# Hybrid decoder layer: the gate projection by Strassen's scheme and ahead of the attentions, and branch products beside branch A's attention

## The chip, the cores and the metric

The kernel runs on one core of a Trainium2 chip. TensorE (PE) multiplies, VectorE (DVE) and ScalarE (ACT) do element-wise work, GpSimd (POOL) and SyncE (SP) issue transfers here. The metric is device time in microseconds (us) of one launch, median of the runs. Program text that sets the order is Python: it writes one list of instructions for each engine, and an engine runs its list in that order.

## What is computed

One layer for 512 tokens and a model width of 2048, all float32. Cut to what matters here:

```python
h = rms_norm(x, norm_g)
(aq, ak, av, az, iq, ik, iw, bcq, bckv, bkpe, bz, cq, cz, gates) = split(h @ w_in)
o_a = dsa_attention(...)     # top 128 of the causal keys by an indexer, 8 heads, relative bias
o_b = mla_attention(...)     # low-rank queries and keys, 8 heads
o_c = memory_attention(...)  # 4 heads over 256 memory tokens, keys from rms_norm(mem) @ w_mem_kv
u = stack([o_a * silu(az), o_b * silu(bz), o_c * silu(cz)])      # each 512 x 1024
y_br = einsum('bsnw,nwd->bsnd', u, w_branch)                     # three products 1024 -> 2048
g = sigmoid(gates.reshape(512, 3, 2048))
merged = einsum('bsnd,bsnd->bsd', g, y_br)
x = x + merged @ w_out
```

The gates are the largest part of the input projection: 2048 x 6144.

## The kernel before

Every large product is made three times: both factors are split into a high and a low part of 12 bits (`split`, line 242: ACT makes the high half, DVE the low one), and high x high, low x high and high x low are summed in PSUM. Such a product is a row of PE of 128x128 by 512 columns. `hh` and `hl` are the halves of h, `whi` and `wlo` those of weights, `uh` and `ul` those of the gated branch outputs, `mh` and `ml` those of the merged sum.

The work of PE is a stream (`stream`, line 259) of chunks; a chunk is 512 columns of one weight matrix, with four PSUM banks of the ring `pg`. For each block k of 128 rows it has 4 x 3 products. SP's queue loads the weights (`wraw`, two blocks of k to a load, 512 KB), and the splits run `LOOK` = 5 blocks ahead. The order of the chunks is written in `build` (line 1269): memory keys and values, latents, queries of C, up-projections of B, keys and values of A, the indexer's queries, queries of A, twelve gate chunks, then three times (branches C, B, A) two chunks of the gate path (`z_chunk`) and four of the branch product (`branch_chunk`), then the output projection.

Between the products of the stream, threads emit the steps of norms and attentions. `run` (line 350) keeps an estimate of every engine's clock: a step is emitted once the products emitted so far outlast what it waits for. A chunk can name a flag (`need`); the stream stops until that flag is set. The first gate-path chunk needs flag "A", the end of branch A's attention. `defer` (line 344) puts element-wise work of a finished chunk a few groups of products later.

A gate chunk's banks are taken out of PSUM by ACT as tanh(x/2), since sigmoid(x) = (1 + tanh(x/2)) / 2, and stored in DRAM (`tanh_to_dram`). `z_chunk` multiplies silu(z) with the attention output, loaded from DRAM, and splits the result into `uh` and `ul`, which stay in SBUF. `branch_chunk` loads the chunk's gates (`y_g`), multiplies them with the bank and adds up the branches in `m`; columns of the weights are on partitions, so after branch A the sum is split as it stands and enters the output projection.

POOL issues all transfers but the weights' loads, in the order in which they are written. Helper lines: every operation goes through a wrapper, so the profile gives all of them line L138; they are told apart by the names of their tiles.

Of the kernel before, what the change touches and what calls it, by code (L numbers as in the profile page):

```python
# [51 lines left out]
PE = object()  # L52


class Engine:
    """An engine's namespace whose calls also advance an estimate of when each tile is written: the
    order in which steps are emitted follows it."""
# [14 lines left out]
class Plan:  # L72
    """Estimated clocks of the engines and of the tiles."""
# [9 lines left out]
    def cost(self, kind, name, out, aps, accum):  # L83
# [3 lines left out]
        if kind == "pe":  # L87
            if name == "transpose":
                return 108
            if aps[1].dtype == BF:  # L90
                return 0.417 * n + 1
            return max(0.417 * n + 2, 108) if n >= 128 else 214
# [59 lines left out]
class Slots:  # L152
    """A tile pool whose tags rotate, with an estimate of when the next slot of a tag is free."""
# [42 lines left out]
class Core:  # L196
    """The core with its engines watched by a plan."""
# [13 lines left out]
def bc(ap, shape, axis):  # L211
    """A broadcast view: a new axis of stride 0."""
    return ap.unsqueeze(axis).to_broadcast(shape)


class Kern:
    LOOK = 5
# [6 lines left out]
    # ---------------------------------------------------------------- helpers  # L224
# [5 lines left out]
    def rsqrt(self, pool, y, v, n):  # L230
        """y = v ** -0.5 on [128, n] (v normal, positive): seed and three Newton steps."""
# [10 lines left out]
    def split(self, hi, lo, src, gain=None):  # L242
        """hi + lo = src * gain, each of 12 bits."""
# [8 lines left out]
    # ---------------------------------------------------------------- the stream of products  # L252
    def chunk(self, w, nk, cols, act, mode, nb, evac, need=None):
        """One block of columns of a product: w [nk*128, cols] in DRAM (or a list of its pieces),
        act(kt) the split activations [128, tokens]. mode "tm": tokens on partitions; "fm": columns on partitions."""
        self.chunks.append(dict(w=w if isinstance(w, list) else [w], nk=nk, cols=cols, act=act, mode=mode,
                                nb=nb, evac=evac, need=need))

    def stream(self):
# [4 lines left out]
        units, loads, lidx = [], [], {}  # L264
        for ci, c in enumerate(self.chunks):
            for k in range(c["nk"]):
                if k % 2 == 0:
                    loads.append((ci, k))
                lidx[ci, k] = len(loads) - 1
                units.append((ci, k))  # L270
        raw, hl = {}, {}
        nload = nsplit = 0

        def load_upto(n):
            nonlocal nload
            while nload < min(n, len(loads)):
                ci, k = loads[nload]
                c = self.chunks[ci]
                r = self.wp.tile([P, 2, 512], F32, name="wraw", tag="wraw", bufs=self.NRAW)
                c0 = 0  # L280
                for w in c["w"]:
                    c1 = c0 + w.shape[1]
                    nc.sync.dma_start(r[:, :, c0:c1], w[k * P:(k + 2) * P, :].rearrange("(k p) c -> p k c", p=P))
                    c0 = c1
                raw[nload] = r
                nload += 1

        def split_upto(n):
            nonlocal nsplit
            while nsplit < min(n, len(units)):  # L290
                ci, k = units[nsplit]
                j = lidx[ci, k]
                load_upto(j + self.NRAW)
                w = self.chunks[ci]["cols"]
                h = self.wp.tile([P, 512], F32R, name="whi", tag="whi", bufs=6)
                l = self.wp.tile([P, 512], F32R, name="wlo", tag="wlo", bufs=6)
                self.split(h[:, :w], l[:, :w], raw[j][:, k % 2, :w])
                hl[ci, k] = (h, l)
                nsplit += 1

        for i, f in enumerate(self.first_loads):
            f()
            load_upto(min(i + 1, self.NRAW))
        yield "boot"

        for i, (ci, k) in enumerate(units):
            c = self.chunks[ci]
            split_upto(i + 1 + min(self.LOOK, i))
            need = c["need"](k) if callable(c["need"]) else c["need"]
            while need and need not in self.flags:  # L310
                yield "stall"
            if k == 0:
                if c.get("pre"):
                    c["pre"]()
                c["ps"] = [self.pg.bank([P, 512]) for _ in range(c["nb"])]
            wh, wl = hl.pop((ci, k))
            ah, al = c["act"](k)
            s, e = k == 0, k == c["nk"] - 1
            for b in range(c["nb"]):
                p = c["ps"][b]  # L320
                if c["mode"] == "tm":
                    n = c["cols"]
                    sl = slice(b * P, (b + 1) * P)
                    mm(p[:, :n], ah[:, sl], wh[:, :n], start=s, stop=False)
                    mm(p[:, :n], ah[:, sl], wl[:, :n], start=False, stop=False)
                    mm(p[:, :n], al[:, sl], wh[:, :n], start=False, stop=e)
                else:
                    m = min(P, c["cols"] - b * P)
                    sl = slice(b * P, b * P + m)
                    mm(p[:m], wh[:, sl], ah, start=s, stop=False)  # L330
                    mm(p[:m], wh[:, sl], al, start=False, stop=False)
                    mm(p[:m], wl[:, sl], ah, start=False, stop=e)
                if e:
                    c["evac"](b, p)
                yield
# [8 lines left out]
    def defer(self, f, last, gap=1):  # L344
        """Do this later: once the chunk's last bank has been read, one after every gap groups of products."""
# [4 lines left out]
    def run(self, main, threads):  # L350
        """Threads yield what their next step waits for: tiles that have to be written, or the name of
        a flag. A step is emitted once the products emitted so far outlast that wait."""
# [25 lines left out]
        def force():  # L378
# [4 lines left out]
            assert c, "deadlock"  # L383
# [17 lines left out]
    # ---------------------------------------------------------------- constants on the chip  # L401
    def setup(self):
        nc, A = self.nc, self.A
        cp = self.cp
        self.g_m = cp.tile([P, KT], F32, name="g_m")
        jp = self.wp.tile([P, 512], I32, name="jp", tag="stage", bufs=5)[:, :P]
# [15 lines left out]
    def small_loads(self):  # L422
        """Gains and constants."""
# [23 lines left out]
    def rotary_tables(self, pool):  # L447
        """cos and sin of position * frequency, tokens on partitions; the position rows for branch A."""
# [126 lines left out]
    # ---------------------------------------------------------------- where the chunks go  # L575
# [4 lines left out]

    def to_dram(self, key, nb, cols, scale=None, sums=()):
        """Write the banks of a chunk to DRAM, [128, nb, cols]. sums: (from, to, dst): dst(b) [128, 1] =
        sum of squares of these columns."""
        nc = self.nc
        dt = self.spill_tile(key, nb, cols)

        def evac(b, p):
            st = self.wp.tile([P, 512], F32, name="stage", tag="stage", bufs=5)
            src, dst = p[:, :cols], st[:, :cols]
# [3 lines left out]
            elif scale is None:  # L593
                nc.vector.tensor_copy(dst, src)
            else:
                nc.vector.tensor_scalar(dst, src, sc, None, op0=OP.mult)
            nc.gpsimd.dma_start(dt[:, b], dst)
# [3 lines left out]
            def squares():  # L601
                for c0, c1, d in sums:
                    junk = self.wp.tile([P, 512], BF, name="junk", tag="junk")
                    nc.scalar.activation(junk[:, :c1 - c0], st[:, c0:c1], AF.Square, accum_out=d(b))
# [6 lines left out]
    def tanh_to_dram(self, key):  # L611
        nc = self.nc
        dt = self.spill_tile(key, 4, 512)

        def evac(b, p):
            st = self.wp.tile([P, 512], F32, name="stage", tag="stage", bufs=5)
            nc.scalar.activation(st, p, AF.Tanh, scale=0.5)
            nc.gpsimd.dma_start(dt[:, b], st)
# [828 lines left out]
```

## Time and profile before

| | |
|---|---|
| median of 3 runs | 1963.02 us (1962.42 to 1963.19) |
| span of the profiled execution | 1961.6 us |
| PE busy | 1946.4 us, 9757 matmuls |
| DVE busy | 1026.6 us |
| ACT busy | 765.9 us |
| data moved | 268.16 MB, mean 137 GB/s |

Busy time of PE counts matmuls that are pipelined, so their durations overlap; what a product costs is its distance from the next. Idle time of an engine that is not the bottleneck costs nothing.

### The profile page before, as it was taken

What the parts mean: (1) busy time and instruction counts of PE and PEld (TensorE: products, weight loads), DVE (VectorE), ACT (ScalarE), POOL (GpSimd) and SP (SyncE); (2) the same over time, 40 slices, a digit from 0 to 9 for tenths busy, and PEclk for the clock granted to TensorE, in tenths of its full rate; (3) what the DMA queues carried; (4) which work ended last, traced back from release to release, by engine and by line L of the source; (5) the groups of instructions that cost most, each with busy time, mean ns of one, the idle gap of its engine ahead of it and who ended that gap; (6) DMA issues with size and microseconds to landing.
All of it is one profiled execution on the core that took longest, in us unless ns stands there. A gap on an engine that the chain in (4) does not pass through costs nothing.

```text
span 1961.6 us, 26146 instructions
## 1 busy us (share of the span) xinstructions
PE 1946.4 (99%) x9757; PEld 1627.1 (83%) x9757; DVE 1026.6 (52%) x2108; ACT 765.9 (39%) x1605; POOL 160.3 (8%) x276
## 2 busy tenths in 40 slices
PE   8999999999999999999999999999999999999999
PEld 6789888888888888888888888888888888888887
DVE  5654425656556668956677652244334544464332
ACT  6644348444455543333333343233223323333221
POOL 1000003111111000020101100000000000000000
PEclk9999999999999999999999999999999999999999
DMA  8735447544344333344433334533433443444442
GB/s 274 241 113 156 132 124 245 166 145 140 108 135 129 116 106 121 112 139 120 128 103 106 116 99 118 162 117 120 162 119 118 139 163 108 128 137 142 141 140 78
DMA packets 121199, 268.16 MB, mean 137 GB/s; under 512 B 12704, under 2 KB 17552, under 8 KB 118512
## 3 DMA queue, kind: packets, MB, share of 16 engines
q1 hardware_dynamic: 99472, 186.80, 31.9%
q0 software_dynamic: 21568, 79.69, 11.9%
q8 instruction: 76, 1.25, 0.3%
q14 instruction: 51, 0.42, 0.1%
q10 hardware_dynamic: 32, 0.01, 0.0%
HBM read 224.74 MB, written 41.71 MB: 136 GB/s over the span
## 4 chain that ended last, share of the span: by engine, by line
PE 94%; DMA 2%; issue 1%; DVE 1%; ACT 1%; POOL 0%; ACTq 0%; POOLq 0%
PE pg L138 85%; PE pb L138 3%; PE pa L138 3%; PE ra L138 2%; DMA wraw<-w_mem_kv 2%; PE rb L138 1%; DVE wlo L138 1%; ACT whi L138 0%; DMA ikw<-sp_bckv 0%; DMA g_rows<-mem_norm_g 0%; ACT junk L138 0%; ACT memh L138 0%; DVE px L138 0%; DMA sp_oC<-c_o 0%; DVE stage L138 0%
## 5 line engine op out<-in xcount | busy, mean ns | idle before, releaser
L138 DVE TENSOR_TENSOR wlo<-wraw,whi 128x512 fp32r<-128x512 f32 (+2 forms) x680 | 461.8, 684 | 744.8 <-ACT whi L138 712.7
L138 ACT ACTIVATE whi<-wraw 128x512 fp32r<-128x512 f32 (+2 forms) x680 | 421.3, 625 | 887.3 <-PE pg L138 814.8
L138 PE MATMUL pg<-hh,whi 128*128 128x512 f32 x1280 | 510.6, 399 | 0.0
L138 PE MATMUL pg<-hh,wlo 128*128 128x512 f32 x1280 | 499.9, 391 | 0.0
L138 PE MATMUL pg<-hl,whi 128*128 128x512 f32 x1280 | 499.1, 390 | 0.0
L138 PEld LDWEIGHTS pg<-hh,wlo 128*128 128x128 f32 x1280 | 240.2, 188 | 51.7
L138 PEld LDWEIGHTS pg<-hl,whi 128*128 128x128 f32 x1280 | 240.9, 188 | 44.1
L138 PEld LDWEIGHTS pg<-hh,whi 128*128 128x128 f32 x1280 | 240.7, 188 | 44.0
L138 PE MATMUL pg<-whi,hh 128*128 128x512 f32 (+1 forms) x448 | 175.3, 391 | 0.4 <-DVE stage L138 0.4
L138 PE MATMUL pg<-whi,hl 128*128 128x512 f32 (+1 forms) x448 | 171.9, 384 | 0.0
L138 PE MATMUL pg<-wlo,hh 128*128 128x512 f32 (+1 forms) x448 | 171.6, 383 | 0.0
L138 PE MATMUL pg<-ul,whi 128*128 128x512 f32 x384 | 149.4, 389 | 0.0
L138 PE MATMUL pg<-uh,whi 128*128 128x512 f32 x384 | 149.4, 389 | 0.0
L138 PE MATMUL pg<-uh,wlo 128*128 128x512 f32 x384 | 149.4, 389 | 0.0
L138 PE MATMUL pg<-wlo,mh 128*128 128x512 f32 x256 | 99.6, 389 | 0.0
L138 PE MATMUL pg<-whi,mh 128*128 128x512 f32 x256 | 99.6, 389 | 0.0
L138 PE MATMUL pg<-whi,ml 128*128 128x512 f32 x256 | 99.6, 389 | 0.0
L138 PEld LDWEIGHTS pg<-whi,hl 128*128 128x128 f32 x448 | 84.1, 188 | 15.5
L138 PEld LDWEIGHTS pg<-whi,hh 128*128 128x128 f32 x448 | 84.3, 188 | 14.3 <-DVE stage L138 0.9
L138 PEld LDWEIGHTS pg<-wlo,hh 128*128 128x128 f32 x448 | 84.3, 188 | 13.1
L138 PEld LDWEIGHTS pg<-uh,whi 128*128 128x128 f32 x384 | 72.1, 188 | 15.0
L138 PEld LDWEIGHTS pg<-ul,whi 128*128 128x128 f32 x384 | 72.1, 188 | 14.9
(343 smaller groups left out, 2366.1 us busy)
## 6 DMA issues: line engine op xcount, KB each, us to landing
wraw<-w_in SPq DMA_DIRECT2D x208, 512.0 KB, 3.6
wraw<-w_branch SPq DMA_DIRECT2D x48, 512.0 KB, 3.7
wraw<-w_mem_kv SPq DMA_DIRECT2D x32, 512.0 KB, 5.1
wraw<-w_out SPq DMA_DIRECT2D x32, 512.0 KB, 3.7
sp_g<-stage POOLq DMA_DIRECT2D x48, 256.0 KB, 3.4
y_g<-sp_g POOLq DMA_DIRECT2D x12, 1024.0 KB, 6.6
px<-x SPq DMA_DIRECT2D x8, 512.0 KB, 6.8
sp_ukv<-stage POOLq DMA_DIRECT2D x16, 256.0 KB, 3.4
```

The costliest lines, as they stand in the source:

```text
L138: return f(*a, **k)
```

## The change

The gates' projection is made by the Winograd form of Strassen's scheme on one level: a chunk now has 1024 columns; h is cut into four quarters (two halves of the tokens by two halves of the 2048 input rows), the weights likewise, and seven products of quarters (P1 to P7) take the place of eight. The sums of quarters of h (S1, S2, S4) are made once, S3 takes the place of a quarter of `hh` and `hl` (kept in DRAM and put back); the sums of the weights' quarters are made for each chunk by DVE, 1024 elements wide. A job is one of the products for two blocks of k, 12 matmuls. P1, P5, P6 and P7 run over all of k first, then P2, P4 and P3; their sums are made when banks are taken out of PSUM.

These six chunks are moved ahead of the attentions, right after the latents. The splits of all weights are 1024 wide and run two jobs ahead. The gate path of C and B is gated at eviction and its halves are stored in DRAM (`sp_u`); that of A is stored as silu(z). When the last product with `hh` and `hl` is done, their place in SBUF is given to a pool (`bp`) that holds `u`, loaded from DRAM by SP's queue for C and B. Branch products of C and B now run beside branch A's attention, have tokens on partitions, and their sum is stored and loaded again (`sp_m0`, `sp_m1`). For branch A, `u_thread` waits for flag "A", loads silu(z) and the attention output and makes `u`; that branch's sum is turned by PE transposes before it is split.

```diff
-    LOOK = 5
+    LOOK = 2
...
+    def strassen_jobs(self, ci, c):
+        w, kp = c["w"][0], c["kp"]
+        quarter = lambda i, j, kb: ([w[:, j * 512:(j + 1) * 512]], (i * kp + 2 * kb) * P)
...
+        nkb = kp // 2
+        for kb in range(nkb):
+            g = {}
+            for p in ("P1", "P5", "P6", "P7"):
...
+            jobs[-4]["raws"] = [quarter(0, 0, kb), quarter(0, 1, kb), quarter(1, 1, kb)]
+        for kb in range(nkb):
+            g = {}
+            for p in ("P2", "P4", "P3"):
...
+            jobs[-3]["raws"] = [quarter(1, 0, kb), quarter(1, 1, kb)]
+        return jobs
...
+        def prep(jb):
+            c, w = jb["c"], jb["cols"]
...
+            g, sh, p, kb = jb["g"], jb["sh"], jb["p"], jb["kb"]
+            if p == "P1":
...
+                g["11"], g["12"], g["22"] = [raw[i] for i in jb["lids"]]
...
+                halves(jb, g["11"], 512)
+                tt(g["11"], g["12"], g["11"], op=OP.subtract)
+            elif p == "P5":
+                tt(sh["T2"][:, 2 * kb:2 * kb + 2], g["22"], g["11"], op=OP.subtract)
+                halves(jb, g["11"], 512)
...
+            elif p == "P6":
+                tt(g["12"], g["22"], g["12"], op=OP.subtract)
...
+                halves(jb, sh["T2"][:, 2 * kb:2 * kb + 2], 512)
+            elif p == "P7":
+                halves(jb, g["12"], 512)
...
+            elif p == "P2":
...
+                t2 = sh["T2"][:, 2 * kb:2 * kb + 2]
+                tt(t2, g["21"], t2, op=OP.subtract)
+                halves(jb, g["21"], 512)
...
+            elif p == "P4":
+                halves(jb, sh["T2"][:, 2 * kb:2 * kb + 2], 512)
+            else:
+                halves(jb, g["22"], 512)
...
+            wh, wl = jb["hl"]
+            if strassen:
...
+                if jb["first"]:
+                    ring = (self.pg, self.pn)[(self.turn + (p in ("P6", "P7"))) % 2]
+                    sets[p] = [ring.bank([P, 512]) for _ in range(2)]
+                    if p == "P7":
+                        self.turn += 1
+                banks = sets[dict(P2="P1", P4="P7", P3="P5").get(p, p)]
...
+                for t in range(2):
+                    for kk in range(2):
+                        k = 2 * kb + kk
+                        for x, (a, b) in enumerate(((0, wh), (0, wl), (1, wh))):
+                            mm(banks[t], op(a, k, t), b[:, kk], start=fresh and k == 0 and x == 0,
+                               stop=jb["last"] and kk == 1 and x == 2, skip_group_check=True)
+                    if jb["last"]:
+                        c["sinks"](p, t, sets)
...
+    def gated_chunk(self, n, c):
+        nc = self.nc
+        dt = self.sp["u%d%d" % (n, c)] = self.dp.tile([P, 2, 4, 512], F32, name="sp_u")
+        key = "ABC"[n]
+        box = {}
+        new = lambda name: self.wp.tile([P, 2, 512], F32, name=name, tag="ev", bufs=4)
+        def act(k):
+            if k == 8:
+                box["o"] = [new("zo") for _ in range(2)]
+                for h, o in enumerate(box["o"]):
+                    nc.gpsimd.dma_start(o, self.sp["o%s%d" % (key, c)][:, 2 * h:2 * h + 2])
+            return self.act_h(k)
+        def evac(b, p):
+            if b % 2 == 0:
+                box["s"] = new("zs")
+            st, o = box["s"], box["o"][b // 2]
+            s = st[:, b % 2]
+            nc.scalar.activation(s, p, AF.Tanh, scale=0.5)
+            nc.vector.scalar_tensor_tensor(s, s, 1.0, p, op0=OP.add, op1=OP.mult)
+            if b % 2 == 0:
+                return
+            def gated():
+                nc.vector.scalar_tensor_tensor(st, st, 0.5, o, op0=OP.mult, op1=OP.mult)
+            def halves():
+                h, l = o.bitcast(F32R), st.bitcast(F32R)
+                self.split(h, l, st)
+                nc.gpsimd.dma_start(dt[:, 0, b - 1:b + 1], o)
+                nc.gpsimd.dma_start(dt[:, 1, b - 1:b + 1], st)
+            self.defer(gated, False, 2)
+            self.defer(halves, b == 3, 1)
+        col = (AZ, BZ, CZ)[n] + c * 512
+        self.chunk(self.A["w_in"][0, :, col:col + 512], KT, 512, act, "fm", 4, evac,
+                   lambda k: key if k == 8 else None)
...
+    def h_ops_thread(self):
...
+            for n, dst, a, b, op in (("S1", r21, r21, r22, OP.add), ("S2", r11, r21, r11, OP.subtract),
+                                     ("S4", r12, r12, r11, OP.subtract)):
+                tt(dst, a, b, op=op)
...
+                self.split(self.s_ops[n][:, 0, ks], self.s_ops[n][:, 1, ks], dst)
+                yield [r]
...
+    def gate_chunk(self, n, c, tail):
...
+            elif p == "P6":
...
+                tt(box["u2"][:, t], sets["P6"][t], box["p1"][:, t], op=OP.add)
...
+                tt(u3[:, t], sets["P7"][t], box["u2"][:, t], op=OP.add)
...
+                tt(u3[:, t], sets["P5"][t], u3[:, t], op=OP.add)
+                tanh(u3[:, t], u3[:, t])
+                if t == 1:
...
+    def u_thread(self):
...
+        yield "z end"
+        for n in (2, 1):
+            self.u[n] = []
...
+                    yield "u2 out %d" % k
+                u = self.bp.tile([P, 2, 2, 512], F32R, name="u", tag="u", bufs=4)
+                self.u[n].append(u)
+                c, b = divmod(2 * k, 4)
+                nc.sync.dma_start(u.bitcast(F32), self.sp["u%d%d" % (n, c)][:, :, b:b + 2])
+                self.flags.add("u%d%d" % (n, k))
...
+            s, o = ahead.pop(0)
+            yield [s, o]
+            nc.vector.scalar_tensor_tensor(s, s, 0.5, o, op0=OP.mult, op1=OP.mult)
+            yield "u1 out %d" % k
+            u = self.bp.tile([P, 2, 2, 512], F32R, name="u", tag="u", bufs=4)
+            self.u[0].append(u)
+            yield [s]
+            self.split(u[:, 0], u[:, 1], s)
+            if k < 2:
+                ahead.append(load(k + 2))
...
     def branch_chunk(self, i, n, c):
...
+            whole = box["g"][b // 2]
+            g = whole[:, b % 2]
+            nc.vector.scalar_tensor_tensor(g, g, 1.0, p, op0=OP.add, op1=OP.mult)
+            if i == 2:
+                m = box["sum"][:, b]
+                self.defer(lambda: nc.vector.tensor_tensor(m, box["m"][b // 2][:, b % 2], g, op=OP.add), b == 3, 1)
+                return
...
+            for d in range(4):
+                def turn(d=d):
+                    pt = ring().bank([P, 512])
+                    for t in range(NT):
+                        nc.tensor.transpose(pt[:, t * P:(t + 1) * P], box["sum"][:, t, d * P:(d + 1) * P], self.ident)
+                    box["pt"] = pt
+                def halves(d=d):
+                    self.split(self.mh[:, 4 * c + d], self.ml[:, 4 * c + d], box["pt"])
+                    self.flags.add("m%d" % (4 * c + d))
+                self.defer(turn, False, 2)
...
+        for c in range(2):
+            self.gated_chunk(2, c)
+        for c in range(2):
+            col = AZ + c * 512
+            self.chunk(win[:, col:col + 512], KT, 512, self.act_h, "fm", 4, self.silu_to_dram("s0%d" % c))
+        for c in range(2):
+            self.gated_chunk(1, c)
+        self.chunks[-1]["post"] = close_h
+        for i in range(2):
+            self.spill_tile("m%d" % i, NT, D)
         for i, n in enumerate((2, 1, 0)):
-            for c in range(2):
-                self.z_chunk(n, c, zcol[n] + c * 512)
-                if i == 0 and c == 0:
-                    self.chunks[-1]["need"] = "A"
-                    f0 = self.chunks[-1]["pre"]
-                    self.chunks[-1]["pre"] = lambda f0=f0: (swap_to_tail(), f0())
             for c in range(4):
                 self.branch_chunk(i, n, c)
```

Three places show how the order of instructions differs. On DVE, in the gate stage of the program before (the last gate chunk):

```order
L138 TENSOR_TENSOR wlo_12021<-wraw_11901,whi_12020 128x512
L138 TENSOR_TENSOR wlo_12039<-wraw_11951,whi_12038 128x512
L138 TENSOR_TENSOR wlo_12055<-wraw_11951,whi_12054 128x512
L138 TENSOR_TENSOR wlo_12073<-wraw_12002,whi_12072 128x512
L138 TENSOR_TENSOR wlo_12089<-wraw_12002,whi_12088 128x512
L138 TENSOR_TENSOR wlo_12107<-wraw_12036,whi_12106 128x512
```

and in that of the program after, for one pair of blocks of k (`sraw` and `wraw` hold quarters of weights, `T2` is a sum kept for the second phase):

```order
L139 TENSOR_TENSOR wlo_2274<-sraw_2082,whi_2273 128x1024
L139 TENSOR_TENSOR wlo_2296<-sraw_2135,whi_2295 128x1024
L139 TENSOR_TENSOR sraw_2135<-wraw_2154,sraw_2135 128x1024
L139 TENSOR_TENSOR T2_2206<-wraw_2188,sraw_2135 128x1024
L139 TENSOR_TENSOR wlo_2316<-sraw_2135,whi_2315 128x1024
L139 TENSOR_TENSOR wraw_2154<-wraw_2188,wraw_2154 128x1024
L139 TENSOR_TENSOR wlo_2337<-T2_2206,whi_2336 128x1024
L139 TENSOR_TENSOR wlo_2353<-wraw_2154,whi_2352 128x1024
```

Low halves alone have become low halves and sums in one queue, each twice as wide. On SP, where the products of the gate path end and those of a branch begin, before:

```order
L138 DMA wraw_14043<-w_in 128x2x512
L138 DMA wraw_14077<-w_in 128x2x512
L138 DMA wraw_14111<-w_branch 128x2x512
L138 DMA wraw_14145<-w_branch 128x2x512
L138 DMA wraw_14179<-w_branch 128x2x512
```

and after:

```order
L139 DMA wraw_12015<-w_branch 128x2x512
L139 DMA wraw_12076<-w_branch 128x2x512
L139 DMA u_12087<-sp_u_134 128x2x1024
L139 DMA u_12089<-sp_u_134 128x2x1024
L139 DMA u_12091<-sp_u_135 128x2x1024
L139 DMA u_12093<-sp_u_135 128x2x1024
L139 DMA wraw_12204<-w_branch 128x2x512
L139 DMA wraw_12275<-w_branch 128x2x512
```

Four loads of `u` of branch C stand between the weights. On POOL, where branch A's attention ends, before (`sp_g` stores a gate chunk, `z_o` loads an attention output):

```order
L138 DMA sp_g01_148<-stage_11873 128x512
L138 DMA sp_oA1_134<-a1_o_11989 128x2x128
L138 DMA sp_g02_149<-stage_12181 128x512
L138 DMA sp_g02_149<-stage_12187 128x512
L138 DMA sp_g02_149<-stage_12193 128x512
```

and after (`yg` is branch B's gated sum, `u_s` and `u_o` are the two factors of branch A's `u`):

```order
L139 DMA sp_oA0_128<-a0_o_14476 128x2x128
L139 DMA sp_m1_141<-yg_14339 128x2x512
L139 DMA sp_m1_141<-yg_14341 128x2x512
L139 DMA sp_oA1_129<-a1_o_14503 128x2x128
L139 DMA u_s_14516<-sp_s00_136 128x1024
L139 DMA u_o_14517<-sp_oA0_128 128x1024
L139 DMA u_s_14520<-sp_s00_136 128x1024
L139 DMA u_o_14521<-sp_oA0_128 128x1024
```

Behind the last stores of the attention stood stores of gates; now the last store of the sum and the loads for branch A stand around it.

## Rows read from the trace of the kernel before

**Rows 1.** The page: span, engines (busy us, share, instructions), the chain by engine.

```profile
span 1961.6 us, 26146 instructions
...
PE 1946.4 (99%) x9757; PEld 1627.1 (83%) x9757; DVE 1026.6 (52%) x2108; ACT 765.9 (39%) x1605; POOL 160.3 (8%) x276
...
PE 94%; DMA 2%; issue 1%; DVE 1%; ACT 1%; POOL 0%; ACTq 0%; POOLq 0%
```

**Rows 2.** The chain in order of time, its longest piece: start us, us, what.

```profile
1184.90 772.51 PE pg L138 x3408
```

**Rows 3.** What PE waited for: us in total, times, longest us.

```profile
PE pb L138 <- DMA g_rows<-mem_norm_g: 4.4, 1, 4.4
PE pb L138 <- DMA px<-mem: 2.4, 1, 2.4
```

**Rows 4.** Windows: stretch, us, busy us of PE, PEld, DVE, ACT, POOL, clock, DMA, GB/s.

```profile
850.00:1130.00 280.00, 280.00 (x1887) 230.61 (x1886) 183.58 (x474) 97.04 (x197) 36.37 (x65) 1.00 0.40 117
0.00:50.00 50.00, 42.15 (x190) 34.43 (x190) 27.72 (x65) 30.79 (x72) 9.53 (x19) 1.00 0.87 276
800.00:850.00 50.00, 50.00 (x237) 41.33 (x236) 47.22 (x102) 17.32 (x35) 2.88 (x5) 1.00 0.39 120
```

**Rows 5.** Timeline of PE, end of the turning of x: start us, us, what.

```profile
108.54 0.60 PE L138 MATMUL pb<-ident,px 128*128 128x128 f32 x4
108.98 0.60 PE L138 MATMUL pa<-ident,px 128*128 128x128 f32 x4
109.70 0.66 PE L138 MATMUL pb<-ident,px 128*128 128x128 f32 x4
111.71 0.63 PE L138 MATMUL pa<-ident,px 128*128 128x128 f32 x4 [1.35 <-DVE hl L138]
```

**Rows 6.** Groups of like instructions of DVE and ACT.

```profile
L138 DVE TENSOR_TENSOR wlo<-wraw,whi 128x512 fp32r<-128x512 f32 x648 | 444.0, 690 | 700.3 <-ACT whi L138 668.2 <-PE pg L138 28.4 <-PE rb L138 2.0
...
L138 DVE TENSOR_TENSOR a_st<-pq,pk 128x1024 bf16<-128x1024 f32 x40 | 48.5, 1213 | 0.0
...
L138 DVE SCALAR_TENSOR_TENSOR y_t<-y_g,pg 128x512 f32<-128x512 f32 x32 | 19.8, 679 | 0.0
...
L138 DVE SCALAR_TENSOR_TENSOR z_t<-z_t,pg 128x512 f32<-128x512 f32 x24 | 16.3, 687 | 1.1 <-ACT z_t L138 1.1
...
L138 ACT ACTIVATE z_t<-pg 128x512 f32<-128x512 f32 x24 | 14.4, 598 | 3.1 <-PE pg L138 1.7
...
L138 ACT ACTIVATE junk<-px 128x1024 bf16<-128x1024 f32 x8 | 8.3, 1042 | 0.0
```

**Rows 7.** Issues of transfers on POOL, like groups.

```profile
L138 POOL DMA_DIRECT2D sp_oA<-a_o x16 | 11.5, 717 | 171.5 <-ACT a_o L138 135.8 <-DVE bm L138 20.9 <-DVE a_sm L138 14.7
...
L138 POOL DMA_DIRECT2D y_g<-sp_g x12 | 6.3, 529 | 384.5 <-DVE z_t L138 283.7 <-DVE y_t L138 67.2 <-DVE m L138 33.6
```

**Rows 8.** Transfers: xcount, KB each, median us from issue to landing.

```profile
y_g<-sp_g POOLq DMA_DIRECT2D x12, 1024.0 KB, 6.6
px<-x SPq DMA_DIRECT2D x8, 512.0 KB, 6.8
...
b_kv<-sp_ukv POOLq DMA_DIRECT2D x8, 512.0 KB, 4.4
```

**Rows 9.** Timeline of PE at its first products.

```profile
9.47 0.63 PE L138 MATMUL pg<-wlo,memh 128*128 128x512 f32 x1
9.90 0.63 PE L138 MATMUL pg<-whi,meml 128*128 128x512 f32 x1
...
11.61 0.40 PE L138 MATMUL pg<-whi,memh 128*128 128x512 f32 x1
11.84 0.40 PE L138 MATMUL pg<-wlo,memh 128*128 128x512 f32 x1
```

**Rows 10.** Windows: the stretch behind the last product.

```profile
1960.00:1962.00 2.00, 0.00 (x0) 0.00 (x0) 0.00 (x0) 0.00 (x0) 0.00 (x0) 0.66 0.00 0
```

**Rows 11.** Windows, instructions with weights' low halves alone: PE, PEld, DVE.

```profile
850.00:1130.00 280.00, 130.39 (x335) 62.69 (x334) 58.28 (x85) 1.00 0.40 117
```

More of the change, by code (lines that the diff above doesn't have):

```diff
@@ L263, in stream @@
         mm = nc.tensor.matmul
-        units, loads, lidx = [], [], {}
+        tt = nc.vector.tensor_tensor
+        jobs = []
         for ci, c in enumerate(self.chunks):
[L266 to L279, printed above, removed]
+            jobs += self.jobs_of(ci, c)
@@ new lines, in stream @@
+        loads, tags = [], {}
+        nstr = 0
+        for ji, jb in enumerate(jobs):
+            jb["lids"] = []
+            for r in jb["raws"]:
+                if "kp" in jb["c"]:
+                    tag = "wraw" if nstr % 6 < 3 else "sraw"
+                    nstr += 1
+                else:
+                    tag = "wraw"
+                tags.setdefault(tag, []).append(len(loads))
+                jb["lids"].append(len(loads))
+                loads.append(dict(src=r, tag=tag, place=len(tags[tag]) - 1, done=False, strassen="kp" in jb["c"]))
@@ new lines, in stream, with load_some @@
+        size = dict(wraw=self.NRAW, sraw=3)
+        raw = {}
+        st = dict(nload=0, nprep=0)
+        def load_some(most):
+            while st["nload"] < len(loads) and most > 0:
+                l = loads[st["nload"]]
+                mine = tags[l["tag"]]
+                if l["place"] >= size[l["tag"]] and not loads[mine[l["place"] - size[l["tag"]]]]["done"]:
+                    return
+                if l["strassen"] and "strassen pool" not in self.flags:
+                    return
+                pool = self.wp if l["tag"] == "wraw" else self.gp
+                r = pool.tile([P, 2, 512], F32, name=l["tag"], tag=l["tag"], bufs=size[l["tag"]])
+                pieces, row = l["src"]
@@ L301, in stream, with done, halves @@
-        for i, f in enumerate(self.first_loads):
+                raw[st["nload"]] = r
+                st["nload"] += 1
+                most -= 1
+        def done(*ids):
+            for i in ids:
+                loads[i]["done"] = True
+                raw.pop(i)
+            load_some(99)
+        def halves(jb, src, w):
+            h = self.wp.tile([P, 2, 512], F32R, name="whi", tag="whi", bufs=3)
+            l = self.wp.tile([P, 2, 512], F32R, name="wlo", tag="wlo", bufs=3)
+            self.split(h[:, :, :w], l[:, :, :w], src)
+            jb["hl"] = (h, l)
@@ L302, in stream, with prep_upto, wait @@
+        def prep_upto(n):
+            while st["nprep"] < min(n, len(jobs)):
+                jb = jobs[st["nprep"]]
+                if "kp" in jb["c"] and "hops" not in self.flags:
+                    return
+                load_some(99)
+                prep(jb)
+                st["nprep"] += 1
+        for f in self.first_loads:
             f()
-            load_upto(min(i + 1, self.NRAW))
+            load_some(1)
         yield "boot"
[L306 to L310, printed above, removed]
-                yield "stall"
-            if k == 0:
+        def wait(need):
+            return need and need not in self.flags
@@ L313, in stream @@
                 if c.get("pre"):
                     c["pre"]()
[L315 to L335, printed above, removed]
+                ring = c.get("ring") or self.pg
@@ L1360, in build @@
                        self.to_dram("ukv%d" % c, 4, 512, sums=sums), "bckvT")
-        sums = [(g * P, g * P + P, lambda b, g=g: one(self.a_ss[:, b], 8 + g)) for g in range(2)]
-        self.chunk(win[:, AK:AK + 512], KT, 512, self.act_h, "tm", 4,
-                   self.to_dram("akv", 4, 512, sums=sums), "kpe")
+        cq_chunk(1)
+        self.chunks[-1]["need"] = "kpe"
         pre(lambda: (lpool.close(), self.flags.add("latents done")))
@@ L1367, in build @@
                        self.to_dram("iq%d" % c, 4, 512))
+        sums = [(g * P, g * P + P, lambda b, g=g: one(self.a_ss[:, b], 8 + g)) for g in range(2)]
+        self.chunk(win[:, AK:AK + 512], KT, 512, self.act_h, "tm", 4, self.to_dram("akv", 4, 512, sums=sums))
         for c in range(2):
```

417 lines of the change are left out of this document (302 added, 115 removed).

## The prediction

> **What bounds the kernel now.** I read the page's engine lines and its chain first, then the chain in order of time, then what TensorE (PE) waited for, then windows by stage. The first should show one full engine: PE is busy 1946.4 of 1961.6 us, VectorE (DVE) half of that, and the chain is 94% PE [rows 1]. The chain's last piece is 3408 products without a break, 772.51 us [rows 2], so a product of 512 columns follows the one before by 772.51 / 3408 = 0.2267 us (the duration that a row of PE gives overlaps its neighbour's and is not the price). PE's two longest waits, 4.4 and 2.4 us, are for the first loads of all [rows 3], and even in the window where DVE is busy 47.22 of 50 us (the top-k search) PE is full [rows 4]. So time falls only where PE gets fewer products, and every new wait of PE is paid in full, since there is no slack on PE to hide it in.
>
> The profiled execution's span is 1961.6 us; the median of the runs is 1963.02, 1.4 us more. The sum is made on the span and 1.4 is added at the end.
>
> **What is removed: 288 products.** Before, the gate projection is 12 chunks of 16 x 4 x 3 = 192 products, 2304. After, six Strassen chunks have 28 jobs of 12 products (4 pairs of k by 7 products), 336 each, 2016. All have 512 columns: -288 x 0.2267 = **-65.3 us**. Counted over the program, PE goes from 9757 matmuls to 9533 (288 fewer, 64 more, next).
>
> **What PE is given.** Branch A's sum now has tokens on partitions and is turned by 64 transposes of 128x128. Four of them start 108.98 - 108.54 = 0.44 us before the next four [rows 5], 0.11 each: **+7.0 us**. Branch products keep their count; that they now have tokens on partitions costs nothing, since the chain of 3408 holds both kinds (branch products with channels, output products with tokens there) without a break.
>
> **The gate stage's new load on DVE.** A Strassen chunk takes PE 336 x 0.2267 = 76.2 us. In it DVE makes 28 low halves and 16 sums of weights, all 1024 wide. The nearest row is a_st, 1213 ns [rows 6]: 44 x 1.21 = 53.2 us. Ten sums read PSUM, 0.68 us each by y_t: 6.8. Together 60 of 76 us; if a 1024-wide operation cost two 512-wide ones (690 ns each), 44 x 1.38 + 6.8 = 67.5. Either fits, and in the first phase (16 jobs, 43.5 us of PE) there are 28 operations, 34 to 39 us. ScalarE (ACT) has 28 x 1.04 (junk<-px, 1024 wide) plus 10 of 0.60, about 35 us. But splits run only two jobs ahead (5.4 us), the sums stand in the same queue as the low halves, and at a chunk's end the PSUM sums are in front of the next chunk's splits. I take 1 us at each of the five joins: **+5 us**, between 0 (the queue never runs dry) and 20 (the 67.5 us with bunching, three us a chunk).
>
> **The first new wait: loading u.** u takes the place of hh and hl, so its load starts after branch B's last gate-path product. On SP's queue it stands behind a weight load that waits for a low half, which on DVE stands behind that chunk's eviction: tanh 0.60, sum 0.69, gating 1.21, low half 1.21, so 3.7 us; then one issue (0.53, y_g's on POOL) and a landing of 1 MB, 6.6 us (y_g) [rows 6 to 8]. Behind the waiting product stand branch A's bias products, so nothing else runs on PE: **+10.8 us**, between 8 (a good part of the eviction already done) and 18 (1 MB at px's rate, 512 KB in 6.8 us, because four such loads and weights go out together: 3.7 + 0.5 + 13.6).
> By the Trainium skill, "DMA: Bandwidth & Descriptors", section "Anatomy of one DMA", a transfer costs about 2 us plus its bytes at 436 GB/s, 4.4 us for 1 MB as an estimate; the trace's 6.6 is higher, and by the page this wait would be 8.6 us and the total 2.2 us less.
>
> **The second new wait: branch A's u.** Branch A's attention ends with the last products of branch B in PE's order (3402 products before the end in the old program, none to spare in the new), and u of branch A is made only from its output. After that last product DVE does one sum, four adds and a low half, 5 x 0.68 + 1.21 = 4.6 us; POOL's queue then issues a store of m (0.53), the last store of A's output (0.72) and the loads of the two factors (0.53 before the second) [rows 7]; 512 KB land in 4.4 us (b_kv) [rows 8]; gating 1.21, high half 1.04, and the third product waits for the low half, 0.75 more. That is 13.8 us, less 12 products of A (1.4) and plus semaphores: **+13 us**, between 9 (the sums of branch B not in the way, 13.8 - 4.6) and 21 (the two factors at px's rate, 13.6 in place of 4.4, less the 1.4).
>
> **The clock.** At the start the first products of 512 columns follow each other by 0.43 us, six of them, then by 0.23 [rows 9]: 1.2 and 2.4 GHz. PE had done little before that. After the last product the granted clock falls to 0.66 of full in the last window [rows 10]. Once PE has begun, the old program has no wait of PE over 2.4 us [rows 3]; the new one gets two of over 10 us, so each may be followed by six slow products, 6 x 0.2 = 1.2 us: **+2.4 us**, between 0 and 5.
> The Trainium skill, "TensorE: Matmul & The Clock Gate", Part 1, says that an array which idled runs at half clock until it has been busy again. The first rows agree; no row before shows it inside the program. Were it wrong, these 2.4 us would go.
>
> **The rest.** (a) Branch A's turn: four chunks, in each of which the first transposes need four PSUM sums, four adds and a low half of DVE (some 4.8 us after the last product with queueing) while PE has about 12 products, 2.7 us, in front: 2.1 each; **+6 us**, 0 to 10. (b) Gated chunks evict by DVE as well as ACT beside the top-k, and branches C and B beside A's attention: **+4 us**, 0 to 15; reasons under the rivals. (c) At the start splits are 1024 wide, and six groups of x's transposes instead of five are left after the last memory product (a group starts 0.4 to 2.0 us after another there [rows 5]): **+2 us**, 0 to 8. (d) Costed at nothing: the spills. u (16 MB both ways), m (16) and a quarter more gate weights (12.6) bring 268 MB to about 313, 160 GB/s over the span, where the start moves 276 [rows 4]; g and m are asked for 48 products, 10.9 us, ahead, landings take 4.4. Without that cover each late g costs its excess, at worst 6.8 us a chunk. Overwriting and restoring hh lies beside products.
>
> Sum: 1961.6 - 65.3 + 7.0 + 5 + 10.8 + 13 + 2.4 + 6 + 4 + 2 = 1946.5; with 1.4, **1948 us**, 0.8% faster. Only a quarter of what is removed stays.
>
> **Rivals.**
> 1. *The small waits are hidden and the two hand-overs cost their lower ends.* For it: in the old program no chunk's join shows a wait. Against: the two waits are dependences. 1961.6 - 65.3 + 7 + 8 + 9 + 1.4 = 1922.
> 2. *Attention A becomes the bound.* From 850 to 1130 us of the old program, beside A's attention, DVE is busy 183.58 of 280 us [rows 4], of which low halves of weights 58.28 [rows 11], so A itself wants 125, 45%. In the new one a branch B chunk (96 products, 21.8 us) wants 4 x 1.21 + 8 x 0.68 = 10.3 us, 47%: together 92%, and the top-k, at 94%, still hid. Mechanism: DVE, in A's last third, with A's flag needed at the first product of branch A. It decides from 100%; A's chain alternates PE, ACT and DVE, so queueing may bring it there sooner. A delay of a tenth of the 280 us goes to PE in full: 28 on top, 1976, slower.
> 3. *DVE bounds the Strassen stage.* For it 67.5 of 76.2 us and a look-ahead of two jobs; against it 60 by the nearer row. Beyond 76.2 each us counts six times; 5 us over in each chunk is 30: 1978, slower.
> 4. *The new waits add up to what is saved*: the upper halves of the terms for u, the turns and evictions, about 15 more: 1963, no change.
> That the change leaves the product count alone is excluded by the order.
>
> **How the numbers follow.** A difference under 0.2% (3.9 us) can't be told from none here. Chances: the forecast 0.54 (its own range 1934 to 1959), rival 1 0.18, rival 4 0.11, rival 2 0.11, rival 3 0.06. Faster 0.72, same 0.11, slower 0.17. The range keeps all but the better tip of rival 1 and the worse half of rivals 2 and 3: 1919 to 1976.
>
> **What would show it.** 9533 matmuls; in the gate stage 336 in 76 us, with DVE near 60. Two pauses of PE over 8 us, one released by the load of u on SP's queue and one by DVE's work on u after loads of POOL; after each some products at 0.43 us. PE waits for DVE before px-like transposes of the merged sum, about 2 us each. Wrong would be: waits for wlo inside the Strassen chunks (rival 3), long waits of A's products on DVE before branch A (rival 2), or no pause at the hand-overs.

## The result, and the profile after

The changed kernel takes 1981.96 us (median of 4 runs, 1979.31 to 1983.06) against 1963.03 of the kernel before: ratio 1.0096, 95% interval 1.0082 to 1.011, so 1% slower, where 0.8% faster was forecast and the range ended at 1976. The page's span, engines and chain answer to [rows 1]:

```profile
span 1980.5 us, 25055 instructions
...
PE 1919.2 (97%) x9533; PEld 1584.4 (80%) x9533; DVE 1245.4 (63%) x1996; ACT 799.1 (40%) x1345; POOL 187.4 (9%) x296
...
PE 88%; DVE 4%; issue 3%; DMA 3%; ACT 2%; POOL 0%; SPq 0%; DVEq 0%; ACTq 0%; POOLq 0%
```

PE has 9533 matmuls, as counted, and is busy 27 us less; the span is 19 us longer, so PE now stands still, or runs slower. What PE waited for (us in total, times, longest), beside [rows 3]:

```profile
PE pn L139 <- ACT u L139: 16.1, 1, 16.1
PE pg L139 <- DMA u<-sp_u: 14.7, 1, 14.7
PE pb L139 <- DMA g_rows<-mem_norm_g: 4.5, 1, 4.5
PE pg L139 <- DVE wlo L139: 4.1, 6, 0.8
PE pg L139 <- DVE stage L139: 3.3, 2, 2.4
PE pg L139 <- DVE zs L139: 2.9, 2, 2.3
```

Both hand-overs are there. The chain in order of time (start us, us, what) shows what the first, behind the last gate-path product at 1435.44, is made of:

```profile
1437.11 1.22 DVE zs L139
1438.33 1.15 DVE wlo L139
...
1439.49 0.37 SPq L139
...
1440.13 10.23 DMA u<-sp_u
...
1450.50 0.77 PE pg L139
```

The 4 us on DVE are those of the forecast; the landing takes 10.2 us where y_g's took 6.6 [rows 8]. All four loads of u are issued here within 3.4 us; branch B's four, issued apart in the same execution, land in 6.3, 7.2, 7.2 and 9.3 us. The second, where the last product of branch A's attention starts at 1681.14:

```profile
1684.56 0.71 POOL sp_m L139
1685.26 0.71 POOL sp_oA L139
...
1686.51 8.57 DMA u_o<-sp_oA
...
1695.18 1.24 DVE u_s L139
...
1696.44 1.06 ACT u L139
```

POOL issues the load behind stores of m (sp_m) that stand ahead of it in its queue, and the landing of 512 KB then takes 8.6 us; two of those stores and three more loads of branch A's factors are under way with it.

The third thing is the clock. Behind the two hand-overs the granted clock (third number from the end) is 0.61 and 0.50 of full, and it is 0.79 in a stretch that begins with a wait of 2.3 us for an eviction:

```profile
1451.00:1455.00 4.00, 4.00 (x29) 3.15 (x28) 2.18 (x6) 0.90 (x2) 0.00 (x0) 0.61 1.03 421
...
1698.00:1702.00 4.00, 3.96 (x10) 2.56 (x10) 2.88 (x3) 1.06 (x1) 1.06 (x2) 0.50 0.73 217
1228.00:1236.00 8.00, 5.73 (x18) 4.01 (x17) 7.53 (x9) 3.29 (x5) 1.07 (x2) 0.79 0.12 13
```

The timeline of PE at that eviction wait (start us, us, what) shows products 0.43 us apart after it, as at the very start [rows 9], so at 1.2 GHz:

```profile
1228.94 0.40 PE L139 MATMUL pg<-hh,wlo 128*128 128x512 f32 x1
1231.61 0.50 PE L139 MATMUL pg<-hh,whi 128*128 128x512 f32 x1 [2.27 <-DVE zs L139]
...
1232.17 0.56 PE L139 MATMUL pg<-hh,wlo 128*128 128x512 f32 x1
1232.53 0.63 PE L139 MATMUL pg<-hh,whi 128*128 128x512 f32 x1
1232.96 0.63 PE L139 MATMUL pg<-hl,whi 128*128 128x512 f32 x1
1233.39 0.63 PE L139 MATMUL pg<-hh,wlo 128*128 128x512 f32 x1
```

The waits that I had listed do not make up the difference, though. All distances between starts of PE from 116 us on, sorted, give (us, of the profiled executions; a product's price is 0.2267):

| | before | after |
|---|---|---|
| products 0.20 to 0.25 us apart | 6918 in 1574.1, mean 0.2275 | 6574 in 1509.7, mean 0.2296 |
| pauses over 0.6 us, beyond a product's price | 1.0 | 45.8 |
| products 0.36 to 0.6 us apart, beyond it | 0 | 7.6 |
| products 0.25 to 0.36 us apart, beyond it | 15.7 | 18.6 |
| turning branch A's sum (64 transposes and their waits) | - | 11.6 |

The first line is the surprise: a product costs 0.0021 us more, 14 us over the program, and no wait shows it.

### The profile page after: what moved, and what is told of

It reads as the page before. It is cut to its first block, busy times and chain, and to the rows that moved or that the text cites. A ratio compares the mean times of both kernels' runs of the same rounds, so it can differ in the third digit from the quotient of the medians.

```text
span 1980.5 us, 25055 instructions
## 1 busy us (share of the span) xinstructions
PE 1919.2 (97%) x9533; PEld 1584.4 (80%) x9533; DVE 1245.4 (63%) x1996; ACT 799.1 (40%) x1345; POOL 187.4 (9%) x296
## 3 DMA queue, kind: packets, MB, share of 16 engines
q0 software_dynamic: 32384, 113.24, 16.4%
## 4 chain that ended last, share of the span: by engine, by line
PE 88%; DVE 4%; issue 3%; DMA 3%; ACT 2%; POOL 0%; SPq 0%; DVEq 0%; ACTq 0%; POOLq 0%
PE pg L139 60%; PE pn L139 18%; PE pb L139 3%; PE pa L139 3%; PE ra L139 2%; DVE wlo L139 1%; DMA wraw<-w_mem_kv 1%; ACT whi L139 1%; PE rb L139 1%; DMA u<-sp_u 1%; DVE m L139 0%; DMA u_o<-sp_oA 0%; DVE yg L139 0%; DVE stage L139 0%; DMA px<-mem 0%
## 5 line engine op out<-in xcount | busy, mean ns | idle before, releaser
L139 DVE TENSOR_TENSOR wlo<-wraw,whi 128x1024 fp32r<-128x1024 f32 (+2 forms) x304 | 367.9, 1211 | 420.0 <-ACT whi L139 419.5
L139 ACT ACTIVATE whi<-wraw 128x1024 fp32r<-128x1024 f32 (+2 forms) x304 | 317.9, 1047 | 544.0 <-PE pg L139 295.0
L139 PE MATMUL pg<-whi,u 128*128 128x512 f32 x640 | 217.1, 401 | 15.9 <-DMA u<-sp_u 14.7
L139 PE MATMUL pg<-whi,hh 128*128 128x512 f32 x576 | 229.9, 399 | 0.0
L139 PE MATMUL pg<-wlo,hh 128*128 128x512 f32 x576 | 225.9, 392 | 0.0
L139 PE MATMUL pg<-whi,hl 128*128 128x512 f32 x576 | 225.3, 391 | 0.0
L139 PE MATMUL pg<-hh,whi 128*128 128x512 f32 x512 | 210.4, 411 | 6.2 <-DVE stage L139 3.3
L139 PE MATMUL pg<-hh,wlo 128*128 128x512 f32 x512 | 203.3, 397 | 0.0
L139 PE MATMUL pg<-hl,whi 128*128 128x512 f32 x512 | 203.2, 397 | 0.0
L139 PEld LDWEIGHTS pg<-hl,whi 128*128 128x128 f32 x512 | 97.3, 190 | 18.8
L139 DVE TENSOR_TENSOR wlo<-sraw,whi 128x1024 fp32r<-128x1024 f32 x60 | 73.3, 1225 | 45.8 <-ACT whi L139 45.8
```

Of the source, the lines that this page charges most:

```text
L139: return f(*a, **k)
```

## The experiments

Ratios are to the kernel before on the same chip; the changed kernel's is 1.0096. In the rows of PE the operand named first is the one of 512 columns; it is said to move, and the other one, of 128x128, to stand.

**e1, right side of SBUF 192 bytes lower.** The allocator puts hh, hl and later u at the upper end; there they begin 224 bytes behind a multiple of 256, while in the kernel before hh and hl begin at 32, and the weights' buffers at 32 in both. The edit puts the right side at 32 as well.

```diff
+        pad = pool("pad", side="right")
+        pad.tile([P, 48], F32, name="pad")
         hpool = ExitStack()
```

> The changed kernel with everything on the right side of SBUF (hh, hl, later u, yg, ym) placed 192 bytes lower, so that these tiles begin 32 bytes behind a multiple of 256, as they do in the kernel before, and not 224. Nothing else changes. Theory 'place': the byte at which a tile begins sets how fast the products that read it follow each other; products with hh (0.229 to 0.233 us apart in the changed kernel) and with u (0.231) go back to 0.227, and the time falls by 14 to 18 us, to 1964 to 1968. Theory 'load' (more work of the other engines and queues stretches the products): spacing and time stay, 1979 to 1984. Theory 'region' (the upper end of SBUF is slower): as 'load', since 192 bytes do not leave it.

Measured: 1969.75 us, ratio 1.0031 (1.002 to 1.0043), 12 us less. The chain of the changed kernel and, below it, of e1 has the same 90 products of the first chunk of C's queries, in which weights move (start us, us, what):

```profile
661.80 20.61 PE pg L139 x90
```

```profile
657.81 20.40 PE pg L139 x90
```

20.61 / 90 = 0.2290 has become 20.40 / 90 = 0.2267. 'Load' and 'region' fall, since no instruction and no queue has changed and the tiles still lie at the upper end; the time is 2 us above what 'place' gave. The kernel is still slower than the one before, so the place is not all that went wrong.

**e2, the same shift in the kernel before.**

```diff
+        self.hp.tile([P, 48], F32, name="pad0")
         hh = self.hp.tile([P, KT, T], F32R, name="hh", tag="hh")
         hl = self.hp.tile([P, KT, T], F32R, name="hl", tag="hl")
+        self.hp.tile([P, 16], F32, name="pad1")
```

> The kernel before with hh and hl (and mh, ml, which take their place) 192 bytes higher, so that they begin 224 bytes behind a multiple of 256 as in the changed kernel; all other tiles keep their offset. Theory 'place': the 3840 products that move hh or hl go from 0.2276 to about 0.233 us, the 1344 that have them as weights to about 0.230; 3840 x 0.0055 + 1344 x 0.002 = 24 us slower, 1980 to 1990. Theories 'load' and 'region': no change, 1962 to 1964.

Measured: 1985.62 us, ratio 1.0116 (1.0099 to 1.0133): 22.5 us for 192 bytes, with the order of every engine unchanged. The last piece of its chain is the one of [rows 2]:

```profile
1195.00 784.18 PE pg L138 x3408
```

The same 3408 products take 784.18 us and not 772.51. So 'place' holds, and this part of what failed in the forecast has nothing to do with Strassen's scheme.

**e6 and e7, whose place?** e6 moves the left side's buffers (weights, sums of h, mh) up by 192 bytes, so that all begin at 224; e7 puts all at a multiple of 256 (56 in place of 48 here, and a pad of 56 on the right side).

```diff
+        lpad = pool("lpad")
+        lpad.tile([P, 48], F32, name="lpad")
         self.wp = pool("wp")
```

> The changed kernel with the pools of the left side from the weights' buffers on (wraw, whi, wlo, the sums of h, mh) 192 bytes higher, so that they begin 224 behind a multiple of 256, as hh, hl and u do; the right side stays. Theory 'own place' (a tile that begins at 224 is slow, whatever the other operand): no product gets faster, those that were at 0.227 go to 0.229 to 0.233, 1984 to 1995. Theory 'relative place' (it is slow when the two operands begin at different places, 224 and 32): all have one place again, spacing 0.227 as in the run with the right side at 32, 1966 to 1971.

> The changed kernel with both sides at a multiple of 256 (left side 224 higher, right side 224 lower). Theory 'own place', if 32 is also a costly place and 0 the free one: products under 0.227, say 0.22, 1900 to 1950. Theory 'relative place', or 'own place' with 32 free already: as with both sides at 32, 1966 to 1971.

Measured: e6 1969.94 us, ratio 1.0035 (1.0021 to 1.005); e7 1972.33, 1.0049 (1.0034 to 1.0064). Both are near e1 (e7 1.3 us above its range): 'own place' falls, and 0 is no better than 32. What counts is how far apart the two operands of a product begin.

**e9 to e11, other distances**: as e1 with 64, 128 and 160 bytes, one run each, so without an interval.

> The changed kernel with the right side 64 bytes lower: hh, hl and u begin 160 behind a multiple of 256, the weights' buffers at 32, so their distance is 128 modulo 256 (it was 192 in the changed kernel, 0 with both sides alike). Theory 'relative place': some pattern of the distance decides; if it repeats at 128, spacing 0.227 as at distance 0, span 1966 to 1971; if it repeats at 256 only, 0.229 to 0.234, 1976 to 1990.

> The same with 128 bytes: distance 64 modulo 256. If the pattern is of lines of 64 bytes, spacing 0.227, span 1966 to 1971; if of 128 or 256, slow products, as in the changed kernel or slower, 1976 to 1990.

> The same with 160 bytes: distance 32 modulo 256 (hh at a multiple of 64). If a distance of half a line of 64 is the costly thing, the slowest of all, spacing 0.233 or more for all kinds, over 1985; if only multiples of 64 that are no multiple of 256 cost, 0.227 and 1966 to 1971.

Measured: 1994.43, 1989.75 and 1994.49 us; e9 is 4 us above the range given for it. The 90 products of e1, in e9 and in e11:

```profile
669.98 20.91 PE pg L139 x90
```

```profile
670.52 20.99 PE pg L139 x90
```

The mean distance of starts (of those from 0.20 to 0.25 us) from the traces:

| hh and hl against the weights' buffers, bytes modulo 256 | runs | hh or hl moves | weights move, hh or hl stand |
|---|---|---|---|
| 0 | before, e1, e6, e7 | 0.2279 to 0.2286 | 0.2275 to 0.2280 |
| 32 | e11 | 0.2331 | 0.2330 |
| 64 | e10 | 0.2298 | 0.2332 |
| 128 | e9 | 0.2327 | 0.2327 |
| 192 | after, e2 | 0.2332 | 0.2295 |

No distance but 0 is free, and a pattern that repeats at 128 bytes, or at every 64, falls; one that repeats at 256 alone is left. The columns differ at 64 and 192 only because the distance is counted from the weights in both. Counted from the standing operand to the moving one, they are one column: 64 bytes gives 0.2298 in e10 (hh moves) and 0.2295 in the changed kernel and e2 (weights move), 192 gives 0.2332 either way, 32, 128 and 224 give 0.2327 to 0.2331. Of the changed kernel's products with unlike places weights move in most, at the mild 64.

**e3, u in the place of hh.** Each quarter of hh takes a part of u as soon as branch B's last gate-path chunk has used it.

```diff
+        place = [self.hh[:, 4 * k:4 * k + 4].rearrange("p (h k) c -> p h k c", h=2) for k in range(4)]
         for n in (2, 1):
             for k in range(4):
-                if n == 1:
-                    yield "u2 out %d" % k
-                u = self.bp.tile([P, 2, 2, 512], F32R, name="u", tag="u", bufs=4)
+                yield "u2 out %d" % k if n == 1 else "hh free %d" % k
+                u = place[k]
```

> The changed kernel, but u is kept in the tile of hh: each quarter of hh is overwritten by a part of u as soon as the last gate-path chunk of branch B has used it, so three of the four loads run beside that chunk. Theory 'dependence' (the 15.1 us pause is only the load that can't start before the last product): the pause falls to under 2 us, the slow products behind it (about 1 us) go too, time falls by 13 to 16 us, to 1966 to 1969. Rival 'moved': the eviction of that chunk on DVE and the weights' halves are late anyway, so that a wait for wlo of 5 us or more takes its place: 1971 to 1977.

Measured: 1955.9 us, ratio 0.9963 (0.9948 to 0.9978), 26 us less than the changed kernel and faster than the kernel before. 'Dependence' holds: no wait for u's load is left. But the time is 10 us below what it gave, and the second hand-over has shrunk as well:

```profile
1683.65 0.50 PE L139 MATMUL pn<-whi,hh 128*128 128x512 f32 x1 [0.21 <-ACT hh L139]
1683.98 0.39 PE L139 MATMUL pn<-wlo,hh 128*128 128x512 f32 x1
1685.43 0.74 PE L139 MATMUL pn<-whi,hh 128*128 128x512 f32 x2 [1.06 <-DVE hh L139]
```

1.4 us where it was 16.4. In the order of PE the attention of branch A ends 84 products (19 us) before branch A's first product, and not right at it. My reading of the program, which no run tests: its own clock of tiles takes hh as one tile, counts a wait for each part of u written into it, and so puts more steps of the attention between the products. These come early now: PE waits 6.0 us in four places for DVE's a_st, in none in the changed kernel.

```profile
PE rb L139 <- DVE a_st L139: 6.0, 4, 2.6
```

Pauses and products of 0.36 to 0.6 us, 53.3 us in the changed kernel, are 26.0 here, about the gain. The run does not tell the load of u apart from that shift by its total, only by its rows.

**e4, branch A's loads ahead.**

```diff
-        yield "A"
-        ahead = [load(0), load(1)]
+        yield "A0 2"
+        ss = [load("s", 0), load("s", 1)]
+        yield "A0 3"
+        ahead = [(ss[0], load("o", 0)), (ss[1], load("o", 1))]
```

> The changed kernel, but for branch A's u the factor silu(z) of the first two parts is loaded ahead, and the attention output of the first four heads is loaded as soon as these heads' last store is issued, ahead of the last stores of m and of the other heads. Theory 'queue' (of the 16.4 us pause, the POOL queue behind DVE's sums is about half): pause 8 to 10 us, time 1973 to 1976. Rival 'DVE' (the sums of branch B's last chunk and the gating on DVE end last): pause 13 us or more, 1978 to 1983.

Measured: 1971.06 us, ratio 1.0038 (1.0023 to 1.0053), 11 us less; better than 'queue' said, because the landing is short too when neither stores of m nor the other three loads go out with it:

```profile
1679.40 0.70 POOL sp_oA L139
1680.11 3.81 DMA u_o<-sp_oA
...
1683.94 1.24 DVE u_s L139
...
1685.20 1.06 ACT u L139
```

From start to start the pause is 5.8 us, so of the 16.4 us some 11 were the queue and what went out beside the load; how much of that were the stores and how much the loads, the run does not tell. Behind it seven products still run 0.41 to 0.67 us apart.

**e5, e1 and e3 together.**

> The changed kernel with both: the right side 192 bytes lower, and u in the place of hh. If the two gains are separate they add up: 1955.9 - 12 to 14 = 1942 to 1945. Rival (the slower products hid waits that now appear): 1948 to 1955.

Measured: 1946.68 us, ratio 0.9918 (0.9903 to 0.9932): 0.45% under e3 (0.9963), about 9 us, of the 12 that e1 alone gave. The time lies between the two ranges, so neither theory is shown. Part of the rest is in the rows: products of 0.36 to 0.6 us cost 6.1 us in the profiled execution of e5 and 1.4 in that of e3.

**e8, three more edits**: besides e4's, the tanh of the last sums of a Strassen chunk is put later and two projections leave PSUM by ACT alone.

```diff
-                tanh(u2[:, t], u2[:, t])
                 if t == 1:
-                    out(u2, 0, 1)
+                    def rest():
+                        tanh(u2, u2)
+                        out(u2, 0, 1)
+                    self.defer(lambda: None, False, 3)
+                    self.defer(rest, True, 1)
```

> The kernel of e5 with three more edits: the tanh of the last sums of a Strassen chunk is put a few groups of products later, so that ACT makes the next chunk's high half first; the odd banks of the indexer's and branch A's projections leave PSUM by ACT and not by DVE; the loads for branch A's u as in e4. Theory: the six joins of 1.26 us fall to under 0.3 (6 us), two of the four waits for evictions beside the top-k (about 2 us) go: 8 us under e5, 1934 to 1938. Rival (DVE is what the joins wait for, ACT's order doesn't matter): joins stay, 1941 to 1945.

Measured: 1947.97 us, ratio 0.9923 (0.9908 to 0.9937), no better than e5, and above both ranges. The joins have shrunk by a third only:

```profile
276.14 0.39 PE L139 MATMUL pg<-whi,hS 128*128 128x512 f32 x1
276.98 0.50 PE L139 MATMUL pg<-wlo,hS 128*128 128x512 f32 x1 [0.45 <-DVE wlo L139]
```

0.84 us where it was 1.26, released by DVE's low half; ACT's order was part of it, DVE's the rest. Against that stand a step of 0.41 us in the middle of each Strassen chunk, 1.1 us in all, and a pause of 3.65 us between the first transposes of branch A's sum, with slow products behind it.

**e12, e5 with the tanh later alone.**

> The kernel of e5 with the tanh of the last sums of a Strassen chunk put later, and nothing else of e8 (there the pause of 3.65 us before the first transposes and the wait of 2.9 us at 1166 us came with the other two edits). Theory: five joins of 0.84 in place of 1.26 us and the product before them at 0.23 in place of 0.40, 3 us under e5: 1942 to 1945. Rival (differences of 2 to 3 us drown in the start's load waits): 1945 to 1949.

Measured: 1945.71 us, ratio 0.991 (0.9893 to 0.9926). It is the best of all runs, 17 us under the kernel before, but within the rival's range, and its interval holds e5's 0.9918; the 3 us are not shown.

## Why the prediction was wrong

The forecast missed by 34 us, in two parts.

**The step that failed** is the price of a product. I took 0.2267 us from [rows 2] for every product of 512 columns, found it in both orientations, and took it over for the new places of tiles at no cost. e2 shows that it is a price of this placement: 3408 products, nothing else changed, 1.5% dearer. In the changed kernel it was 14 us (0.0021 x 6574); e1 gave back 12. None of the rivals held it either.

**The sizes that were off.** The other 20 us are terms of the sum whose mechanisms were there, and most cost more than I took:

| term | forecast | measured |
|---|---|---|
| 288 products fewer | -65.3 | -65 at 0.2267 |
| 64 transposes and the wait of the turn | 7.0 + 6 | 11.6 |
| joins of Strassen chunks | 5 | 7 (the first chunk's start and five joins, 0.9 to 1.0 each, and a slow product before) |
| load of u | 10.8 | 14.8 |
| branch A's u | 13 | 16.3 |
| slow clock after pauses | 2.4 | 6.7 |
| evictions beside top-k and attention | 4 | 8.3 (2.4 and 2.6 the longest) |
| start | 2 | 2.5 |
| products' place | 0 | 14 |

The measured ones add up to about +16; some 3 us more are small distances (0.25 to 0.36 us), and the span grew by 18.9. The landings were above the rows that I took, 6.6 and 4.4 us for a load by itself, and inside the bounds of 13.6: 10.2 us for the first of four loads of 1 MB at once, 8.6 for 512 KB behind stores. For the clock I counted two pauses; two eviction waits of 2.7 and 2.8 us from start to start were followed by products at 0.43 us as well, five joins of 1.26 us were not, and the term ended above its bound of 5. The turn of branch A's sum waits otherwise than I wrote: not 2 us before the first transposes, but three waits of 0.27 us for DVE's adds in each chunk. Without the 14 us of the place the time would have been about 1968, still not faster than before; so the place alone does not explain the wrong sign.

**What held.** The gate stage is not bound by DVE (rival 3): a chunk takes 78.1 us of the trace where I had 76.2 and a join of 1, and DVE is busy 58.5 of them (I had 60). Rival 2 fell: PE waits nowhere for the attention's chain in the changed kernel; that its span is near that rival's 1976 is chance. Rival 1 fell: both hand-overs cost more than I took, not their lower ends. That e5 comes to 1946.68, near the forecast, is chance too: there the hand-overs are all but gone and other waits have come. Rival 4, the sum of larger waits, describes the 20 us, 5 more than it gave; alone it would have ended near 1968, where e1 is.

The rule of the Trainium skill on the clock ("TensorE: Matmul & The Clock Gate", Part 1), that an array which idled runs at half clock until it has been busy again, is borne out inside a program by the rows behind the pauses of 15 and 16 us: granted 0.61 and 0.50, then 1.00. The Trainium skill's price of a transfer ("DMA: Bandwidth & Descriptors", section "Anatomy of one DMA", stated there for those that GpSimd issues) makes 4.4 us for 1 MB as an estimate; on SP's queue 10.2 were measured, further off than the rows' 6.6.

## What to carry to other kernels

A price per instruction read from a trace belongs to the placement of its operands too: when a change moves tiles to another side or pool of SBUF, compare where the two operands of the hot matmuls begin, modulo 256, before and after, and make them alike with a few bytes of padding. On an engine that was full, each of the two new hand-overs through DRAM cost its whole chain, and the landing must be priced with everything that goes out at the same time. Either free the target in parts, so that the load starts early, or put independent products between, as e3 did by both.

## What the runs showed of the hardware that was not expected

Two operands of a float32r matmul that begin at different places modulo 256 bytes cost 0.001 to 0.006 us of 0.227 per product of 512 columns (table above); why, no run here tells. It goes by the distance from the standing operand to the moving one: 64 bytes is mild (0.2295 to 0.2298), 32, 128, 192 and 224 are not (0.2327 to 0.2332).

Behind two pauses of PE of 2.67 and 2.83 us the changed kernel ran six or seven products at half the clock. That is no rule: the same two pauses in e3 left the granted clock at 1.00 (1230 to 1234 us and 1329 to 1334 us), and e12 has none behind 2.67 us and seven behind 2.99. What decides is not shown.
